# Reordering two second products of an expert around a branch, and making two transposes together

## The chip, the cores and the metric

The kernel runs on one core of one Trainium2 chip. The metric is the device time of one execution in microseconds (us). TensorE is called PE in the profile, its weight loads PEld, VectorE DVE, ScalarE ACT, GpSimd POOL, SyncE SP; a name with a q (PEq, DVEq) is that engine's sequencer, which issues instructions and executes branches.

## The reference

One layer of a decoder for 256 prompt rows and 32 sample rows (288 tokens of 1024 numbers). A convolution and a state-space branch come first; the change lies in what follows them, a mixture of 32 experts, of which each token uses 4:

```python
logits = (t @ w_r + b_r).astype(jnp.float32)
top_val, top_idx = lax.top_k(logits, TOP_K)
gates = jax.nn.softmax(top_val, axis=-1)
for e in range(N_EXPERTS):
    gu = t @ w1[e] + b1[e]
    g = jnp.minimum(gu[:, :D_FF], SWIGLU_LIMIT)
    up = jnp.clip(gu[:, D_FF:], -SWIGLU_LIMIT, SWIGLU_LIMIT)
    act = g * jax.nn.sigmoid(SWIGLU_ALPHA * g) * (up + 1.0)
    out = out + comb[:, e:e + 1] * (act @ w2[e] + b2[e])
```

Everything is float32. An expert's weights are 12 MB, read from memory once; 32 experts are 403 MB.

## The kernel before, in words

`moe` goes through the experts in order. For each it computes only the tokens that were routed to it, in blocks of 32. How many there are is known on the device alone, so the blocks stand under nested branches on a register (`tc.If(reg > 32 * b)`), and every engine takes these branches in its own sequencer. With these inputs 20 experts have at most 32 tokens. Experts 4, 8, 12, 14 and 26 have 33 to 64 (two blocks, 0 and 1); experts 7, 10, 19, 28 and 29 have 65 to 96 (blocks 0 to 2), and 13 and 24 have 129 to 160 (blocks 0 to 4). Blocks 0 and 1 of two neighbouring experts share one tile of 128 rows, `ysp`; blocks from 2 on are the expert's extras and have a tile `ysx` of their own.

A block's work is:

- the gate product `ff1` (line 1216): 68 matmuls on TensorE into one PSUM bank (block 0: bank A; odd blocks: C; even ones: B), and then `silu` on VectorE and ScalarE, which leaves `acts[b]`;
- the transposes `act_tr` (line 1224): two transposes of `acts[b]` on TensorE into bank D and one ScalarE copy into a tile of `ats`;
- the second product `ff2` (line 1234): 64 matmuls (records `y`, line 1243) from `ats` and the second weights into one bank (block 0: C, odd: A, even: B), and then four copies into 32 rows of `ysp` or `ysx` (line 1249), ScalarE and VectorE by turns and one after the other.

`fill` puts a piece of other work in the middle of a product: `{4: ...}` ahead of the fifth of eight steps. `scatter` (line 1257) multiplies `ysp` or `ysx` with a table of gates that VectorE makes (`gates`, line 1251), in matmuls `sc` and `ss` (extras: `sc_x`, `ss_x`), and VectorE adds the result to `acc` and `accs` (lines 1268, 1278).

The order of an expert's work on every engine is written out by hand (the schedule is manual). `ph1` (line 1328): the nest "a" with the gate products of blocks 1 and up, then block 0's gate product with block 1's transposes in it. Then, where `e` is even, the scatter of the two experts before; then the list of the extra tokens of the next expert (`lists`, records `li`, line 1166) and their fetch. `ph2` (line 1341): the nest "b" with the second products of blocks 1 and up:

```python
with tc.If(reg > 32 * b, label=f"{half}{e}_{b}"):
    if b < 5:
        hint(e, reg, half, b + 1)
    end = f(b)
    if b < 5:
        rest(e, reg, half, f, b + 1)
    if end:
        end()
```

Here `f(b)` is block b's second product with the transposes of block b + 1 in its middle, and `end` the scatter of the extras, which block 2 returns. So the order is: product 1, branch on 64, gates and product 2, branch on 96, product 3 and so on, then the scatter. `hint` (line 1307) tells the sequencers ahead of time which way a branch will go (a compare at line 1309 and a hint instruction). In the program a body stands right behind its branch; a branch whose condition doesn't hold goes to a short block behind the body, which only brings the semaphores up to date. After `ph2`: the load of the next expert's count with the first hint for it (`tokens`, line 1311), for even `e` a table of gates and the list of the expert after the next (a one-hot tile `S_None` on VectorE, line 1158, then `li` on TensorE), block 0's transposes, and block 0's second product. Bank C of that product is the one that block 1 of the next expert needs.

SyncE loads the weights in pieces of 1 MB into a ring; a piece's slot is loaded again when the last product that reads it is done (`done`, line 1144). The second weights are released after block 0's second product, which is the last of an expert.

Of the kernel before, what the change touches and what calls it, by code (L numbers as in the profile page):

```python
# [37 lines left out]
NE = 32  # L38
# [1064 lines left out]
def moe(tc, sb, wring, pm, ident, iotaj, h2, h2d, h2off, cm, posm, cnt, b1s3, sel, place, acc, accs, w1, w2, tail, pre, ln_rows, first, final):  # L1103
# [5 lines left out]
    def at_(o, shape, name):  # L1109
        return sb.mem.at(o, shape, F32, name)  # L1110

    def bank(tag, name):
        return pm.tile([P, 512], F32, tag=tag, bufs=1, name=name)
# [4 lines left out]
    acts = [at_(o + 1024 * j, [P, 256], f"acts{2 * i + j}") for i, o in enumerate((o_ac, o_ac2, o_ac2 + 2048)) for j in range(2)]  # L1118
    ats = [at_(o + 1024 * j, [P, 256], f"at{2 * i + j}") for i, o in enumerate((o_sg, o_atx)) for j in range(2)]
# [4 lines left out]
    ysp = at_(o_yp, [P, 1024], "ysp")  # L1124
    ysx = at_(o_y1, [P, 1024], "ysx")
# [61 lines left out]
    def columns_x(nm, m):  # L1187

        r = slice(64 * m, 64 * m + 64)
        tp = pm.tile([P, 8, 64], F32, tag="m", bufs=2, name=f"gt{nm}")  # L1190
        for k in range(8):
            nc.tensor.transpose(tp[:, k], gsx[r, P * k:P * k + P], ident[r, r])
        nc.scalar.copy(htx[:, :, r], tp)

    def silu(nm, a, g, m=0):

        g1 = at_(o_g1 + 1024 * m, [P, 256], f"g1{nm}")
        nc.vector.tensor_scalar_min(g1, g[:, 0:256], 7.0)
        sg = at_(o_sg + 1024 * m, [P, 256], f"sg{nm}")
        nc.scalar.activation(sg, g1, AF.Sigmoid, scale=1.702)  # L1200
        nc.vector.tensor_scalar(a, g[:, 256:512], -7.0, 7.0, op0=ALU.max, op1=ALU.min)
        nc.vector.scalar_tensor_tensor(a, a, 1.0, g1, op0=ALU.add, op1=ALU.mult)
        nc.vector.tensor_tensor(a, a, sg, op=ALU.mult)

    def ff1_mm(e, h, w, outs, fill={}):

        for c, (o, tp) in enumerate(outs):
            nc.tensor.matmul(o, sel[0:96, e:e + 1].to_broadcast([96, w]), b1v[0:96, :, c, :], start=True, stop=False, tile_position=tp)  # L1208
        for k in range(8):
            if k in fill:  # L1210
                fill[k]()
            wk = wt[e][k].rearrange("p u (c n) -> p c u n", c=4)
            for c, (o, tp) in enumerate(outs):
                nc.tensor.matmul(o, h[:, k], wk[:, c], start=False, stop=k == 7, tile_position=tp)

    def ff1(e, b, fill={}):

        gu = bank("ABC"[b and 1 + b % 2], f"gu_{e}_{b}")
        outs = [(gu[32 * c:32 * c + 32, :].rearrange("p (u n) -> p u n", u=2), (0, 32 * c)) for c in range(4)]
        h = htx[:, :, 32 * b - 64:32 * b - 32] if b > 1 else ht[:, :, 64 * (e % 2) + 32 * b:64 * (e % 2) + 32 * b + 32]  # L1220
        ff1_mm(e, h, 32, outs, fill)
        silu(f"_{e}_{b}", acts[b], gu, b % 2)

    def act_tr(nm, bs, tag="D"):

        tp = bank(tag, f"at{nm}")
        for m, (a, t) in enumerate(bs):
            for h in range(2):
                o = 256 * m + 128 * h
                nc.tensor.transpose(tp[:, o:o + P], a[:, h * P:h * P + P], ident)  # L1230
        for m, (a, t) in enumerate(bs):
            nc.scalar.copy(t, tp[:, 256 * m:256 * m + 256])  # L1232

    def ff2(e, b, ys, r, fill={}):

        y = bank("CBA"[b and 1 + b % 2], f"y_{e}_{b}")
        at = ats[b if b < 2 else 2 + b % 2]
        for kt in range(8):
            if kt in fill:
                fill[kt]()  # L1240
            c, h = kt // 2, kt % 2
            for q in range(4):
                nc.tensor.matmul(y[32 * q:32 * q + 32, 0:256], at[:, h * P + 32 * c:h * P + 32 * c + 32],  # L1243
                                 wt[e][8 + c][:, h, 256 * q:256 * q + 256], start=kt == 0, stop=kt == 7, tile_position=(0, 32 * q))
        for q in range(4):
            i, s = slice(32 * q, 32 * q + 32), slice(256 * q, 256 * q + 256)
            if e + 1 == NE and b < 2:
                nc.vector.tensor_tensor(wt[NE][0][r:r + 32, 0, s], y[i, 0:256], wt[NE][1][i, 0, s], op=ALU.mult)  # L1248
            (nc.vector.tensor_copy if q % 2 and b else nc.scalar.copy)(ys[r:r + 32, s], y[i, 0:256])  # L1249

    def gates(o, nm, tab):

        g = at_(o, [P, 288], f"gst{nm}")
        nc.vector.tensor_scalar(g, iotaj[:, 0:288], tab[0][:, 0:1], tab[0][:, 1:2], op0=ALU.is_equal, op1=ALU.mult)
        return g

    def scatter(nm, gst, ys, gated=False):

        for t in range(2):
            for n in range(2):  # L1260
                sc = pm.tile([P, 512], F32, tag="sc", bufs=2, name=f"sc{nm}_{t}_{n}")
                nc.tensor.matmul(sc, gst[:, t * P:t * P + P], ys[:, n * 512:n * 512 + 512], start=True, stop=True)  # L1262
                a = acc[:, t, n * 512:n * 512 + 512]
                if gated:
                    u = at_(o_g1, [P, 512], f"u{nm}_{t}_{n}")
                    nc.vector.tensor_tensor(u, sc, wt[NE][1][:, 0, n * 512:n * 512 + 512], op=ALU.mult)
                    sc = u
                nc.vector.tensor_tensor(a, a, sc, op=ALU.add)  # L1268
        ss = pm.tile([P, 512], F32, tag="sc", bufs=2, name=f"ss{nm}")
        for c in range(4):  # L1270
            nc.tensor.matmul(ss[32 * c:32 * c + 32, 0:256], gst[:, 256:288], ys[:, c * 256:c * 256 + 256],
                             start=True, stop=True, tile_position=(0, 32 * c))
        ss = ss[:, 0:256]
        if gated:
            u = at_(o_atx, [P, 256], f"us{nm}")
            nc.vector.tensor_tensor(u, ss, wt[NE][1][:, 1, 256:512], op=ALU.mult)
            ss = u
        nc.vector.tensor_tensor(accs, accs, ss, op=ALU.add)
# [28 lines left out]
    def hint(e, reg, half, b):  # L1307

        tc.mark_branch_hint_location(f"{half}{e}_{b}", hint=reg > 32 * b, engines=engs)

    def tokens(e):

        reg = nc.values_load(cnt[32:33, e:e + 1], engines=with_pool, min_val=0, max_val=288)
        hint(e, reg, "a", 1)
        return reg

    def rest(e, reg, half, f, b=1):
# [10 lines that stand above are left out]
    def ph1(e, reg):  # L1328

        def f(b):  # L1330
            if b in (2, 4):
                columns_x(f"_{e}_{b}", b // 2 - 1)
            ff1(e, b)
            if b == 5:
                with tc.If(reg > 192):
                    more(e, reg)
        rest(e, reg, "a", f)
        hint(e, reg, "b", 1)
        ff1(e, 0, {5: lambda: act_tr(f"_{e}_1", [(acts[1], ats[1])])})

    def ph2(e, reg):

        def f(b):
            end, fill = None, {}
            if b == 2:
                nm = f"_{e}_x"
                gst = gates(o_g, nm, tabs[2 + e % 2])

                def end():
                    scatter(nm, gst, ysx, e + 1 >= NE)  # L1350
            if b < 5:
                fill[4] = lambda: act_tr(f"_{e}_{b + 1}", [(acts[b + 1], ats[2 + (b + 1) % 2])])
            ff2(e, b, *((ysp, 64 * (e % 2) + 32) if b == 1 else (ysx, 32 * b - 64)), fill)
            return end
        rest(e, reg, "b", f)
        return None if e + 1 == NE else tokens(e + 1)

    steps = pre()
# [8 lines left out]
    with tc.manual_schedule(engines={ENG.PE, ENG.DVE, ENG.Activation, ENG.Pool}):  # L1367
        s, sx = onehot(0, o=o_sg), onehot(0, 64)
        reg = tokens(0)
# [11 lines left out]
        for e in range(NE):  # L1381
            last, j = e + 1 == NE, e // 2
            if not last:
                s = onehot(e + 1, 64)
            ph1(e, reg)
            done(e, range(8))
            if e % 2 == 0 and e:
                scatter(f"_{e}", gst, ysp)
            if not last:
                lists(e + 1, s, tabs[2 + (e + 1) % 2], 0)  # L1390
                fetch(gsx, tabs[2 + (e + 1) % 2])
            reg = ph2(e, reg)
            if e:
                step()
            if e == 1 or e and e % 2 == 0:
                gst = gates(o_gst, f"_{e}", tabs[j % 2])
# [319 lines left out]
```

## Time and profile before

| | |
|---|---|
| Median of 3 runs | 1482.36 us (1478.8 to 1483.93) |
| The profiled execution | 1484.18 us; its span 1482.4 us, 1.8 us lie around it |
[...]
| TensorE busy | 1173.1 us (79% of the span) |
| VectorE, ScalarE, GpSimd busy | 523.7, 298.1, 277.3 us |
| Data moved by DMA | 473.22 MB, mean 319 GB/s |

The first 340 us or so belong to the stage before the experts. In the profile, "idle before" is the time in which an engine did nothing ahead of an instruction, and the name behind the arrow is what ended it. An instruction of which parts overlap its neighbours (matmuls do) has a time that is longer than what it adds to the engine's path; the distance between starts says that. Branches of the sequencers have records of their own, with times; they aren't counted as busy.

### The profile page before, as it was taken

To read this page: it belongs to the slowest core of one execution; us is meant where nothing else is said; L and a number is where in the kernel's file an instruction comes from. 1 tells how busy PE (TensorE), PEld (TensorE's weight loads), DVE (VectorE), ACT (ScalarE), POOL (GpSimd) and SP (SyncE) were. 2 spreads that over 40 slices of the span, in tenths; PEclk is the share of its full clock that TensorE was granted. 3 is DMA by queue.
4 is the path that set the end of the run, shared out by engine and by line. 5 is a ranking of instruction groups with operands and counts; after the bars stand their busy time and mean duration, and the time that the engine had idled before them with its cause. 6 is when DMAs were issued, how large, how long until landed. Compare 5 with 4: busy or idle time off the path is not lost. (4 is left out here: it accounts for less than half of the span.)

```text
span 1482.4 us, 25892 instructions
## 1 busy us (share of the span) xinstructions
PE 1173.1 (79%) x10262; PEld 592.5 (40%) x10262; DVE 523.7 (35%) x1057; ACT 298.1 (20%) x624; POOL 277.3 (19%) x237
## 2 busy tenths in 40 slices
PE   4888788886778768888779977778777897778975
PEld 0777677853323323333323433333323233223332
DVE  6789898752222122212221321212202122213124
ACT  2634645520101101111101111111011011111111
POOL 4676865621100000000000000000000000000022
PEclk8889889997799789989889998889888998999998
DMA  9465646578799999998793589999999957997683
GB/s 393 164 228 147 221 148 244 216 288 318 283 414 413 411 413 414 380 364 346 308 398 120 229 342 363 412 413 412 414 414 412 381 230 282 414 415 283 262 334 125
DMA packets 91769, 473.22 MB, mean 319 GB/s; under 512 B 14406, under 2 KB 15774, under 8 KB 52560
## 3 DMA queue, kind: packets, MB, share of 16 engines
q1 hardware_dynamic: 81264, 459.68, 78.1%
q0 software_dynamic: 7328, 6.55, 1.6%
q8 instruction: 167, 2.74, 0.7%
q10 hardware_dynamic: 2912, 3.46, 0.7%
q14 instruction: 98, 0.80, 0.2%
HBM read 485.33 MB, written 4.28 MB: 330 GB/s over the span
## 5 line engine op out<-in xcount | busy, mean ns | idle before, releaser
L1176 POOL DMA_INDIRECT gs1.360_2956<-h2d,tab3.366_2962 x16 | 15.9, 993 | 558.9 <-DVE tab3.366_2962 L1172 350.9
L1249 ACT COPY ysp.368_2964<-y 32x256 f32<-32x256 f32 x152 | 55.2, 363 | 186.5 <-PE y L1243 173.9
L1176 POOL DMA_INDIRECT gs1.360_2956<-h2d,tab2.365_2961 x16 | 16.0, 1001 | 344.7 <-DVE tab2.365_2961 L1172 154.5
L1208 PE MATMUL gu<-b1h.19_79,sel.17_76 96*32 96x512 bf16 x220 | 23.2, 410 | 71.9 <-PEq L1319 44.2
L567 DVE SCALAR_TENSOR_TENSOR v.103_627<-cb.73_324,pk.20_89,v.103_627 128x256 f32<-128x256 f32 x60 | 54.7, 911 | 1.5
L1232 ACT COPY at1.356_2952<-at 128x256 f32<-128x256 f32 x32 | 11.9, 372 | 206.8 <-PE at L1230 206.8
L1232 ACT COPY at0.355_2951<-at 128x256 f32<-128x256 f32 x32 | 11.9, 373 | 200.2 <-PE at L1230 199.7
L1230 PE MATMUL at<-consts.1_57,acts0.349_2945 128*128 128x128 f32 x64 | 17.7, 371 | 39.8 <-issue 32.0
L1208 PEld LDWEIGHTS <-sel.17_76 96*32 96x32 bf16 x220 | 7.0, 93 | 97.7 <-issue 96.1
L1268 DVE TENSOR_TENSOR acc.345_2940<-acc.345_2940,sc 128x512 f32<-128x512 f32 x60 | 39.8, 683 | 11.9 <-PE sc L1262 11.9
L1268 DVE TENSOR_TENSOR acc.345_2940<-acc.345_2940,sc_x 128x512 f32<-128x512 f32 x28 | 19.2, 687 | 27.3 <-PE sc_x L1262 27.3
L1249 DVE COPY ysp.368_2964<-y 32x256 f32<-32x256 f32 x24 | 10.2, 423 | 52.6 <-ACT ysp.368_2964 L1249 52.6
L1185 DVE COPY ht.361_2957<-gt 128x512 f32<-128x512 f32 x16 | 11.1, 692 | 49.9 <-PE gt L1184 49.9
L1230 PEld LDWEIGHTS at<-consts.1_57,acts0.349_2945 128*128 128x128 f32 x64 | 10.4, 212 | 43.2 <-issue 38.9
L1184 PE MATMUL gt<-consts.1_57,gs0.359_2955 128*128 128x128 f32 x120 | 23.6, 362 | 0.0
L1176 POOL DMA_INDIRECT gs0.359_2955<-h2d,tab1.364_2960 x8 | 7.9, 991 | 78.2 <-DVE tab1.364_2960 L1168 70.6
L1184 PEld LDWEIGHTS gt<-consts.1_57,gs0.359_2955 128*128 128x128 f32 x120 | 20.7, 193 | 0.3 <-issue 0.2
L1249 DVE COPY ysx.369_2965<-y 32x256 f32<-32x256 f32 x22 | 9.3, 421 | 30.7 <-ACT ysx.369_2965 L1249 30.7
L1232 ACT COPY at2.357_2953<-at 128x256 f32<-128x256 f32 x14 | 5.2, 372 | 70.7 <-PE at L1230 70.7
L1230 PEld LDWEIGHTS at<-consts.1_57,acts1.350_2946 128*128 128x128 f32 x64 | 6.4, 141 | 26.8 <-issue 26.8
L1176 POOL DMA_INDIRECT gs0.359_2955<-h2d,tab0.363_2959 x7 | 6.9, 992 | 48.1 <-DVE tab0.363_2959 L1168 48.1
L1230 PE MATMUL at<-consts.1_57,acts1.350_2946 128*128 128x128 f32 x64 | 14.0, 301 | 0.0
(3009 smaller groups left out, 2946.5 us busy)
## 6 DMA issues: line engine op xcount, KB each, us to landing
wada_0.21_91<-in_w_ada_dram SPq DMA_DIRECT2D x1, 1024.0 KB
wada_1.22_93<-in_w_ada_dram SPq DMA_DIRECT2D x1, 1024.0 KB
wada_2.24_97<-in_w_ada_dram SPq DMA_DIRECT2D x1, 1024.0 KB
wada_3.25_99<-in_w_ada_dram SPq DMA_DIRECT2D x1, 1024.0 KB, 12.7
wada_4.26_101<-in_w_ada_dram SPq DMA_DIRECT2D x1, 1024.0 KB
wada_5.27_103<-in_w_ada_dram SPq DMA_DIRECT2D x1, 1024.0 KB
wada_6.28_105<-in_w_ada_dram SPq DMA_DIRECT2D x1, 1024.0 KB
wada_7.29_107<-in_w_ada_dram SPq DMA_DIRECT2D x1, 1024.0 KB
```

The source lines that it names most:

```text
L567: V.scalar_tensor_tensor(vt_(j), cb[:, j, k:k + 256], wd[:, k, j:j + 1], vt_(j), op0=ALU.mult, op1=ALU.add)
L1176: nc.gpsimd.indirect_dma_start(out=g, out_offset=None, in_=h2d, in_offset=bass.IndirectOffsetOnAxis(ap=tab[1], axis=0), bounds_check=287, ...
L1184: nc.tensor.transpose(tp[:, i], gs[:, P * (4 * h + i):P * (4 * h + i) + P], ident)
L1185: (nc.vector.tensor_copy if h else nc.scalar.copy)(ht[:, 4 * h:4 * h + 4], tp)
L1208: nc.tensor.matmul(o, sel[0:96, e:e + 1].to_broadcast([96, w]), b1v[0:96, :, c, :], start=True, stop=False, tile_position=tp)
L1230: nc.tensor.transpose(tp[:, o:o + P], a[:, h * P:h * P + P], ident)
L1232: nc.scalar.copy(t, tp[:, 256 * m:256 * m + 256])
L1249: (nc.vector.tensor_copy if q % 2 and b else nc.scalar.copy)(ys[r:r + 32, s], y[i, 0:256])
L1268: nc.vector.tensor_tensor(a, a, sc, op=ALU.add)
```

## The change

Block 1's transposes, which lay in block 0's gate product, now take block 2's with them (`acts[1:3]` into `ats[1:3]`), for every expert, whether it has a block 2 or not. The nest "b" becomes: branch on 32, then at once the branch on 64. If there are more than 64 tokens: gates, product 2, the branches on 96 and up with their products, then block 1's second product, and then the scatter of the extras. If there are not: an else arm with block 1's second product alone. That product now stands twice in the program and has no transposes in it.

```diff
-        ff1(e, 0, {5: lambda: act_tr(f"_{e}_1", [(acts[1], ats[1])])})
+        ff1(e, 0, {5: lambda: act_tr(f"_{e}_1", list(zip(acts[1:3], ats[1:3])))})
 
     def ph2(e, reg):
 
+        def first():
+            ff2(e, 1, ysp, 64 * (e % 2) + 32)
+
         def f(b):
-            end, fill = None, {}
-            if b == 2:
+            fill = {}
+            if b < 5:
+                fill[4] = lambda: act_tr(f"_{e}_{b + 1}", [(acts[b + 1], ats[2 + (b + 1) % 2])])
+            ff2(e, b, ysx, 32 * b - 64, fill)
+
+        with tc.If(reg > 32, label=f"b{e}_1"):
+            hint(e, reg, "b", 2)
+            with tc.If(reg > 64, label=f"b{e}_2") as two:
+                hint(e, reg, "b", 3)
                 nm = f"_{e}_x"
                 gst = gates(o_g, nm, tabs[2 + e % 2])
-
-                def end():
-                    scatter(nm, gst, ysx, e + 1 >= NE)
-            if b < 5:
-                fill[4] = lambda: act_tr(f"_{e}_{b + 1}", [(acts[b + 1], ats[2 + (b + 1) % 2])])
-            ff2(e, b, *((ysp, 64 * (e % 2) + 32) if b == 1 else (ysx, 32 * b - 64)), fill)
-            return end
-        rest(e, reg, "b", f)
+                f(2)
+                rest(e, reg, "b", f, 3)
+                first()
+                scatter(nm, gst, ysx, e + 1 >= NE)
+            with two.Else():
+                first()
         return None if e + 1 == NE else tokens(e + 1)
```

## Rows read from the trace of the kernel before

**Rows 1.** The page: slices of the span, busy tenths; a group of section 5.

```profile
DMA  9465646578799999998793589999999957997683
...
L1268 DVE TENSOR_TENSOR acc.345_2940<-acc.345_2940,sc_x 128x512 f32<-128x512 f32 x28 | 19.2, 687 | 27.3 <-PE sc_x L1262 27.3
```

**Rows 2.** Stretches: length, busy us by engine (instructions), clock, DMA share, GB/s.

```profile
851.00:1151.00 300.00, 231.46 (x2072) 96.97 (x2068) 61.85 (x166) 35.67 (x92) 14.87 (x15) 0.87 0.98 396
```

**Rows 3.** Waits of TensorE, 400 to 1482 us: total, times, longest.

```profile
PE gu L1208 <- PEq L1319: 43.3, 22, 5.0
PE at L1230 <- issue: 32.0, 9, 4.1
...
PE sc_x L1262 <- PEq L1319: 11.8, 3, 4.5
...
PE sc_x L1262 <- DVEq L1319: 8.0, 4, 2.1
...
PE gu L1214 <- DMA w_7.640_9292<-in_w_dram: 1.5, 1, 1.5
```

**Rows 4.** Branches of line 1319, 400 to 1482 us: ns shortest/median/longest, first and last start.

```profile
L1319 PEldq COMPARE_BRANCH  x132: 67/192/6258, 397.9 to 1453.0; - x132
```

**Rows 5.** Timeline of TensorE, expert 8, around block 1's second product: start, us, work.

```profile
621.29 1.07 PE L1243 MATMUL y<-w_8.679_10236,at1.356_2952 128*32 128x256 f32 x16
...
623.15 0.44 PE L1230 MATMUL at<-consts.1_57,acts2.351_2947 128*128 128x128 f32 x2
...
624.41 1.05 PE L1243 MATMUL y<-w_11.682_10242,at1.356_2952 128*32 128x256 f32 x16
629.10 1.44 PE L1166 MATMUL li<-cm.14_73,S_None.724_11485 128*128 128x4 f32 x6 [3.64 <-DVE S_None.724_11485 L1158]
```

**Rows 6.** The branch on 64 alone, experts 4, 8, 12, 14, 26: ns, start.

```profile
L1319 PEldq COMPARE_BRANCH  x1: 2483/2483/2483, 475.9 to 475.9; - x1
L1319 PEldq COMPARE_BRANCH  x1: 2791/2791/2791, 624.0 to 624.0; - x1
L1319 PEldq COMPARE_BRANCH  x1: 4383/4383/4383, 770.4 to 770.4; - x1
L1319 PEldq COMPARE_BRANCH  x1: 6236/6236/6236, 880.1 to 880.1; - x1
L1319 PEldq COMPARE_BRANCH  x1: 4232/4232/4232, 1283.2 to 1283.2; - x1
```

**Rows 7.** Expert 8: branches from 619 to 628 us; the hint's compare.

```profile
L1319 PEldq COMPARE_BRANCH  x3: 83/192/2791, 620.0 to 627.0; - x3
...
L1309 PEldq ALU_OP  x1: 37/37/37, 620.2 to 620.2; - x1
```

**Rows 8.** Timeline of VectorE, expert 8, behind block 1's second product.

```profile
625.91 0.42 DVE L1249 COPY ysp.368_2964<-y 32x256 f32<-32x256 f32 x1 [4.11 <-ACT ysp.368_2964 L1249]
...
628.49 0.55 DVE L1158 TENSOR_TENSOR S_None.724_11485<-consts.1_57,posm.15_74 128x384 f32<-128x384 f32 x1
```

**Rows 9.** Timeline of TensorE, products and scatter of the extras, experts 7 and 29.

```profile
574.71 1.07 PE L1243 MATMUL y<-w_8.641_9294,at1.356_2952 128*32 128x256 f32 x16 [0.37 <-ACT sg_0.677_10229 L1200]
...
581.79 1.05 PE L1243 MATMUL y<-w_11.644_9300,at2.357_2953 128*32 128x256 f32 x16
586.95 5.43 PE L1262 MATMUL sc_x<-ysx.369_2965,gst_x.686_10321 128*128 128x512 f32 x8 [4.11 <-PEq L1319]
...
1411.06 3.86 PE L1262 MATMUL sc_x<-ysx.369_2965,gst_x.1500_30827 128*128 128x512 f32 x8 [1.94 <-DVEq L1319]
```

**Rows 10.** Timeline of TensorE, the list behind block 1's product, experts 4, 12, 14, 26.

```profile
480.96 1.45 PE L1166 MATMUL li<-cm.14_73,S_None.576_7759 128*128 128x4 f32 x6 [3.62 <-DVE S_None.576_7759 L1158]
...
776.20 1.43 PE L1166 MATMUL li<-cm.14_73,S_None.872_15211 128*128 128x4 f32 x6 [4.30 <-DVE S_None.872_15211 L1158]
...
887.71 1.44 PE L1166 MATMUL li<-cm.14_73,S_None.946_17074 128*128 128x4 f32 x6 [6.15 <-DVE S_None.946_17074 L1158]
...
1288.83 0.82 PE L1166 MATMUL li<-cm.14_73,S_None.1390_28252 128*128 128x4 f32 x6 [4.13 <-DVE S_None.1390_28252 L1158]
```

## The prediction

> **What bounds the kernel now.** I read the page's slices first, then the stretches, then TensorE's waits, then single branches. In the expert stage the DMA engines are full in many slices [rows 1], 98% busy over the 300 us of experts 14 to 23 [rows 2]. Yet TensorE almost never waits for a weight: of its waits after 400 us the largest on a DMA is 1.5 us [rows 3], and with the smaller ones, all at experts 6, 7 and 24, I count some 7 us. So TensorE's own order sets the pace, and the ring of weights can take up about 7 us of any delay. What TensorE does wait for is its sequencer at the branches: 43.3 us before a first matmul of the next gate product, 32.0 us ahead of transposes with no other cause shown, and 11.8 + 8.0 us before the scatter of extra sums [rows 3].
>
> A branch of PE's sequencer takes between 67 and 6258 ns, median 192 [rows 4]. The short ones fall through into the block that stands next; the long ones skip a block of code. Row by row, the branch on 64 tokens in the five experts with 33 to 64 tokens took 2.5, 2.8, 4.4, 6.2 and 4.2 us [rows 6]. It is issued some 4 us after its hint: for expert 8 the hint's compare stands at 620.2 [rows 7] and the branch at 624.0 [rows 6], the second product lying between. So the target arrived 6.4 to 10.2 us after the hint. That is the quantity on which all else rests.
>
> **Part 1: the else arm, experts 4, 8, 12, 14, 26.** Before, the branch on 64 waits behind the second product. TensorE works through that product meanwhile (623.15 to 625.46 is its second half), and the next list starts at 629.10, after 3.64 us of waiting for VectorE [rows 5]. That wait is VectorE's: its copies of the product begin at 625.91 and its one-hot ends at 629.04 [rows 8], so about 3.5 us follow any second product, whatever the branch does. After the change the hint stands where it stood, but the branch on 64 follows it at once, and the product stands behind the branch. The code arrives when it did before; what covered the wait now comes after it. Expert 8: branch end 624.0 + 2.8 = 626.8, then the product. Two of these take 574.71 to 582.84, 8.1 us [rows 9], so 4.1 each, less 0.4 for the transposes no longer in it. I add 1.5 because TensorE has idled: the scatter that followed a 4.11 us gap took 5.43 us, one after 1.94 us took 3.86 [rows 9], and I take that difference for the product as an estimate. With 0.3 us of starting and 3.6 of VectorE the next list comes 9.1 us after the branch's end: 635.9 instead of 629.10, +6.8. In the same way expert 4: 475.9 + 2.5 + 9.1 = 487.5 instead of 480.96, +6.5; expert 12: +7.7; 14: +7.7; 26: +7.7 [rows 6, 10]. Sum 36.4 us. Some comes back: the next expert's first branch gets its hint earlier against TensorE's work, and a part of the 43.3 us [rows 3] lies there; I estimate 6 us for experts 5, 9 and 27. Net +30. Bounds: without the cold clock 7 less; with a second block of code that has to arrive in the middle of the product, up to some 2 us each, 10 more.
>
> [...]
>
> **Part 2: the other arm, experts 7, 10, 13, 19, 24, 28, 29** (28 additions, four each [rows 1]). The scatter's matmul waited 4.11 us in expert 7 and 1.94 in expert 29 [rows 9]; over the seven it is 11.8 + 8.0 = 19.8 us [rows 3]. About 2 us of each is the copies of the last extra product, which the change lays under the moved product; the rest is the branch on 96, which stays between the products and now leaves its gap ahead of the moved one. Its hint moves 4 us earlier, as does the work behind it, and in odd experts somewhat more, since the sequencer runs ahead there. I keep 8 us of gaps (2 in expert 7, 3 in 10, 1 in 19, 2 in 28) and so save 12. The odd experts also lose a wait of 0.4 us ahead of the second product, as that product's bank is the first gate product's: 4 x 0.4, some 2 us. Saved 14; bounds 5 (only experts 13, 24 and part of 29 win) and 24 (all gaps go and the scatter runs warm). The other queues cost nothing: no list, DMA issue or weight release changes its place, and VectorE's table of gates only moves ahead of a product for which it waits anyway.
>
> At the end of this arm a jump over the else body is new, seven times. Nothing in the trace shows one of that length by itself; between 0.2 us (the median branch) and 2.5 (the shortest of the five above) I take 0.3, as the skipped code is one product long and the code behind it follows in order: 2 us, bounds 1 and 17.
>
> **Part 3: transposes made together.** Two transposes cost TensorE 0.4 us [rows 5]. In the 12 larger experts they move. In the other 20 they are new, with one ScalarE copy that nothing waits for. In the 12 odd ones TensorE then waits for a branch anyway (the 32.0 us [rows 3]); the 8 even ones pay: 3 us. If that cover is gone, 7 us.
>
> **Sum.** 30 - 14 + 2 + 3 = 21, less 7 us that the ring takes up (TensorE's waits for weights shrink by that): +14. The profiled execution took 1484.2 us, its span 1482.4; the median of the runs shown is 1.8 us below it. 1484.2 + 14 = 1498; between the two bases I say 1497.
>
> **Rivals.** *The branch is cheap (faster).* If the else arm is at hand when the branch comes, or arrives within the 1.3 us that the sequencer is ahead (in expert 8 its branch on 32 stands at 620.0 [rows 7], the product behind it at 621.29 [rows 5]), the five experts pay nothing: their waits for the list, 3.6 + 3.6 + 4.3 + 6.1 + 4.1 us [rows 5, 10], shrink to 3.5 each (-4), the transposes leave (-2), hints come earlier (-6). With -14 and +3 that is -23: 1461. It decides wherever the stall is under about 2 us. Against it: all five branches to that target were longer. For it: the target lies elsewhere in the new code. [...] Chance 0.13.
>
> *The fetch starts at the branch, not at the hint (no change).* The branch comes 4 us earlier than it did, so the code also does, and part 1 falls by 20 to 10 us: 10 - 14 + 2 + 3 - 3 = -2, 1482. For it: expert 14's branch alone took 6.2 us. Against: the branches of experts 4 and 8 ended 2.5 and 2.8 us after their start, too soon for a fetch that began with them, if 6.2 us is one. Chance 0.18.
>
> *Second fetches (slower still).* The else product straddles a block in most of the five, and the new jump stalls in all seven: +10 and +15, 1522. Chance 0.17. My forecast keeps 0.52.
>
> **Numbers.** A measurement of this kernel tells about 0.3% (4.5 us) from no change. The range 1470 to 1524 leaves out most of the first rival and the tail of the last; the likeliest case alone spans 1484 to 1515. Slower: 0.17 + 0.47; same: 0.12 + 0.05; the rest, 0.19, faster.
>
> **What would show it.** In the changed profile TensorE's second product in experts 4, 8, 12, 14 and 26 has an idle time of 5 to 9 us before it, put down to PE's sequencer, and some branches of 6 to 10 us; the waits for the list stay at 3.5. The scatter's matmuls wait for nothing, and gaps of 0 to 3 us stand ahead of the moved product. If the second product of those five experts starts right behind the list, part 1 is wrong and the first rival holds.

## The result and the profile after

The changed kernel takes 1532.84 us (median of 4 runs, 1528.49 to 1534.52) against 1482.49 us before (4 runs): a ratio of 1.0308, 95% interval 1.0269 to 1.0348. It is slower, as forecast, but by 50 us where 15 were forecast, and outside the range by 9 us. The profiled execution took 1528.49 us, its span is 1526.7 us; that is 44.3 us more than the span before, and these 44.3 us are what is to be found below.

First the page. TensorE's line, the DMA slices, the instruction queue (q8: packets, MB, share) and VectorE's additions of the extras:

```profile
PE 1184.1 (78%) x10302; PEld 603.2 (40%) x10302; DVE 523.3 (34%) x1057; ACT 301.8 (20%) x644; POOL 277.5 (18%) x237
...
DMA  9457456567999998697992669999999849995681
...
q8 instruction: 174, 2.85, 0.8%
...
L1268 DVE TENSOR_TENSOR acc.345_2940<-acc.345_2940,sc_x 128x512 f32<-128x512 f32 x28 | 18.6, 686 | 5.8 <-PE sc_x L1262 5.5
```

TensorE is busy 11 us longer (1173.1 before) on the same matmuls and 40 more small transposes. The run with the transposes alone (below) is busy for 1177.0 us, so some 7 us of the 11 are matmuls that took longer; in the five products behind the else arm (below) the granted clock was 0.50 to 0.80 of full speed. The DMA slices look as they did [rows 1]; there is no new transfer, but 7 more instruction packets (167 before). VectorE's idle time ahead of the extras fell from 27.3 us [rows 1] to 5.8: that wait of the scatter is indeed gone.

Next, TensorE's waits from 400 us on (total, times, longest):

```profile
PE gu L1208 <- PEq L1319: 41.3, 22, 5.1
PE at L1230 <- issue: 29.4, 9, 4.0
PE y L1243 <- issue: 28.0, 9, 5.5
...
PE y L1243 <- PEq L1319: 11.7, 4, 4.8
PE gu L1214 <- issue: 10.2, 6, 3.1
...
PE y L1243 <- DVEq L1319: 5.8, 3, 1.9
PE gt L1184 <- issue: 5.7, 2, 3.0
PE y L1243 <- DMA w_4.540_7017<-in_w_dram: 5.6, 1, 5.6
...
PE y L1243 <- DMA w_0.719_11456<-in_w_dram: 5.5, 1, 5.5
PE y L1243 <- DMA w_0.941_17261<-in_w_dram: 5.4, 1, 5.4
...
PE sc_x L1262 <- DVE acc.345_2940 L1268: 4.4, 7, 0.7
...
PE gu L1214 <- DMA w_7.530_6619<-in_w_dram: 0.7, 1, 0.7
```

Before, the rows of "issue" ahead of the gate and second products were:

```profile
PE gu L1214 <- issue: 6.0, 3, 2.8
...
PE y L1243 <- issue: 3.5, 3, 1.3
```

Read against [rows 3]: the 19.8 us of `sc_x` on sequencers are gone, 4.4 us on VectorE's additions are left. In their place `y` waits, which before had only those 3.5 us of "issue" and no wait for a sequencer or a DMA. Five of these waits, 5.4 to 5.6 us each, stand ahead of block 1's product in experts 4, 8, 12, 14 and 26; three of the five carry the name of a weight's DMA, two are among the nine of "issue". The name of the DMA is only the last event that the profile saw. The branches on 64 show the cause, one row for each of the five:

```profile
L1354 PEldq COMPARE_BRANCH  x1: 6282/6282/6282, 471.4 to 471.4; - x1
L1354 PEldq COMPARE_BRANCH  x1: 6257/6257/6257, 626.0 to 626.0; - x1
L1354 PEldq COMPARE_BRANCH  x1: 6250/6250/6250, 771.4 to 771.4; - x1
L1354 PEldq COMPARE_BRANCH  x1: 6112/6112/6112, 891.3 to 891.3; - x1
L1354 PEldq COMPARE_BRANCH  x1: 6077/6077/6077, 1300.1 to 1300.1; - x1
```

Each took 6.1 to 6.3 us, against 2.5 to 6.2 before [rows 6], and each product begins some 0.3 us behind its branch. In each of these waits one packet of the instruction queue lands, about 1.5 us before the branch ends (in expert 8 at 630.7, the branch's end at 632.3, in the trace's packet records). In the larger experts, where the same branch goes on to the next block, it took 0.07 us (the trace's branch records).

TensorE's timeline in expert 4, from the list ahead of block 1's product to the list behind it:

```profile
471.52 0.83 PE L1166 MATMUL li<-cm.14_73,S_64.543_7023 128*128 128x2 f32 x6
477.90 1.93 PE L1243 MATMUL y<-w_8.531_6621,at1.356_2952 128*32 128x256 f32 x16 [5.56 <-DMA w_4.540_7017<-in_w_dram]
...
483.00 1.26 PE L1243 MATMUL y<-w_11.534_6627,at1.356_2952 128*32 128x256 f32 x16
487.32 1.44 PE L1166 MATMUL li<-cm.14_73,S_None.576_7939 128*128 128x4 f32 x6 [3.06 <-DVE S_None.576_7939 L1158]
```

The product starts 5.56 us late, takes 6.4 us from 477.90 to the end of its last row at 484.26, and then the wait of 3.06 us for VectorE's one-hot stands where it stood [rows 10]. The granted clock of that product (a stretch: length, PE, PEld, DVE, ACT, POOL busy, clock, DMA share, GB/s):

```profile
477.90:484.30 6.40, 6.35 (x64) 3.15 (x64) 0.00 (x0) 0.00 (x0) 0.00 (x0) 0.57 1.01 412
```

Behind an idle time of 5.56 us the granted clock is 0.57 of full speed, near the lower of the two levels in the trace's clock records, 0.5 and 1; the same product without a gap ahead took 3.7 us at a granted clock of 1.00 in another kernel (arms swapped, below), so the cold clock costs 2.7 us and not the 1.5 estimated.

In the larger arm, the moved product of expert 28:

```profile
1383.65 0.64 PE L1243 MATMUL y<-w_8.1419_29841,at1.356_2952 128*32 128x256 f32 x8 [2.25 <-PEq L1319]
1389.14 1.08 PE L1243 MATMUL y<-w_8.1419_29841,at1.356_2952 128*32 128x256 f32 x8 [4.85 <-issue]
```

The moved product waits 2.25 us for the branch on 96, runs 8 matmuls, and then stops for 4.85 us in the middle with no cause but "issue": a packet on the instruction queue ended 1.4 us before it went on. The same happened in experts 19 (4.17 us) and 7 (1.22), and in the else product of experts 8 (2.09) and 26 (1.59). Stops inside a group, all rows of "issue" but the one ahead of `at`, less the two gaps of 5.5 and 5.4 counted above: 28.0 - 10.9 + 10.2 + 5.7 = 33 us, against 6.0 + 3.5 = 9.5 us before.

Last, where the moved product of expert 13 waits:

```profile
852.22 1.07 PE L1243 MATMUL y<-w_8.863_15318,at1.356_2952 128*32 128x256 f32 x16 [1.94 <-DVEq L1319]
```

It waits for VectorE's sequencer and not for a branch of TensorE's own; experts 10 and 24 have the same row. (In expert 10 TensorE's own branch on 96, of 2.83 us, ended only 0.6 us earlier, so there VectorE adds little.) The product writes to bank A, which blocks 3 and 5 use inside the nest; so at the nest's end TensorE waits for VectorE, whose last work before that is to copy the extra product out (in expert 13 until 852.02). This is the wait that the scatter had [rows 9], moved one product ahead.

**The sum.** Idle time on TensorE: five gaps +27.3, the moved product's waits 11.7 + 5.8 = +17.5, stops inside groups +23.5; scatter -15.4, lists of the five 21.7 to 15.5 [rows 5, 10], -6.2; weights 7.0 to 0.7, -6.3; gate products and transposes behind a branch 75.3 to 70.7, -4.6. With 11 us more of busy time that is +46.8, and 44.3 were measured; the 2.5 us between are smaller waits that were not summed.

The same by place, which the experiments are compared by: stretch E is from the list ahead of block 1's product to the next list, summed over the five experts with an else arm (46.5 us before); stretch L is from the first second product of the nest to the end of the scatter of extras, over the seven larger experts (130.3 us before). Both are differences of starts and ends in TensorE's timeline, as shown for expert 4 (471.52 to 487.32: 15.8 us; before 472.42 to 480.96: 8.5). The span is given against 1482.4 us. All three are of one profiled execution each, which can lie some us off its kernel's median (that of "else arm alone" and that of "bank C, hint lost" are the slowest of their kernels). The kernel before was timed again beside the runs below and took 1486 to 1488 us there, so their span column holds 3 to 6 us that are not theirs; the ratio compares with these times, and what is said of faster and slower goes by it. Block 2's transposes lay in E and L before and lie in neither after (nor in "transposes alone"): a second product took 4.16 us with them (expert 8) and takes 3.66 without, so waits and stops grew by some 0.5 us more in each of the 12 experts than E and L show. With that, two kernels that can't be told from the one before, transposes alone and code shifted, show how far the sums stray: E by 1 us, L by 5.

| kernel | E | L | span | time ratio, interval |
|---|---|---|---|---|
| the change | +36.6 | +10.4 | +44.3 | 1.0308, 1.0269 to 1.0348 |
| transposes alone | -2.9 | +1.6 | +9.8 | 1.0024, 0.9985 to 1.0064 |
| else arm alone | +43.2 | -5.3 | +50.6 | 1.0241, 1.0200 to 1.0282 |
| change, bank C | +34.5 | +10.4 | +41.4 | 1.0257, 1.0215 to 1.0299 |
| before, code shifted | +0.9 | +4.8 | +10.7 | 1.0023, 0.9995 to 1.0051 |
| change, early hint | +25.4 | +16.8 | +38.7 | 1.0245, 1.0212 to 1.0279 |
| early hint, bank C | +13.4 | +6.8 | +14.3 | 1.0123, 1.0097 to 1.0150 |
| both hints early, bank C | +24.4 | +24.5 | +46.0 | 1.0268, 1.0244 to 1.0291 |
| change, arms swapped | +5.5 | +22.2 | +37.1 | 1.0222, 1.0181 to 1.0262 |
| bank C, hint lost | +37.0 | +19.2 | +72.1 | 1.0373, 1.0307 to 1.0438 |
| before, early hint | +8.0 | +14.0 | +22.6 | 1.0109, 1.0074 to 1.0144 |
| bank C, product joined | +40.5 | +2.7 | +38.6 | 1.0232, 1.0171 to 1.0293 |

### The profile page after: what moved, and what is told of

Its sections match the earlier page's. It is cut to its first block, busy times and chain, and to the rows that moved or that the text cites. A ratio compares the mean times of both kernels' runs of the same rounds, so it can differ in the third digit from the quotient of the medians.

```text
span 1526.7 us, 25981 instructions
## 1 busy us (share of the span) xinstructions
PE 1184.1 (78%) x10302; PEld 603.2 (40%) x10302; DVE 523.3 (34%) x1057; ACT 301.8 (20%) x644; POOL 277.5 (18%) x237
## 5 line engine op out<-in xcount | busy, mean ns | idle before, releaser
L1249 DVE COPY ysp.368_2964<-y 32x256 f32<-32x256 f32 x24 | 10.2, 423 | 120.7 <-ACT ysp.368_2964 L1249 120.7
L1184 PE MATMUL gt<-consts.1_57,gs0.359_2955 128*128 128x128 f32 x120 | 22.6, 346 | 5.7 <-issue 5.7
L1201 DVE TENSOR_SCALAR acts0.349_2945<-gu 128x256 f32<-128x256 f32 x32 | 13.3, 415 | 0.0
```

The costliest lines, as they stand in the source:

```text
L1184: nc.tensor.transpose(tp[:, i], gs[:, P * (4 * h + i):P * (4 * h + i) + P], ident)
```

## The experiments

The theory behind them: the else arm's far jump costs most, and what is moved in the larger arm hides nothing. The rivals: the transposes, the new layout of the code as such, the bank alone, or the second copy of the product.

**Transposes alone.** Of the change only the common transposes; the old order of the products and their single copy stay. Against the changed kernel:

```diff
             hint(e, reg, "b", 2)
+            first()
             with tc.If(reg > 64, label=f"b{e}_2") as two:
...
-                first()
                 scatter(nm, gst, ysx, e + 1 >= NE)
-            with two.Else():
-                first()
```

> Only the transposes are made together; block 1's product stands ahead of the branch on 64 again and there is no else arm. Theory 1 (the far else arm carries the loss): 1482 + 3 = 1485 us (1478 to 1492), and the sum of the waits ahead of the lists and of the scatter as before, 22 and 20 us. Rival (a shifted program and more transposes carry it): over 1500 us.

1.0024, the interval holding 1 (10 runs). The lists of the five wait 21.4 us, as expected, the scatter 24.8 where 20 were expected. The term of +3 us (1.002) stands within what can be told; the transposes are not the loss.

**Else arm alone.** Against the changed kernel: block 1's product stands first in both arms, so the larger experts keep the old order.

```diff
         with tc.If(reg > 32, label=f"b{e}_1"):
             hint(e, reg, "b", 2)
             with tc.If(reg > 64, label=f"b{e}_2") as two:
...
+                first()
                 f(2)
                 rest(e, reg, "b", f, 3)
-                first()
                 scatter(nm, gst, ysx, e + 1 >= NE)
             with two.Else():
                 first()
```

> Both arms begin with block 1's product, so only the branch on 64 moves ahead of it; the scatter waits as before. Theory 1: the five experts of the else arm still idle 5 to 5.6 us each ahead of block 1's product, 27 us in all, and 1505 to 1518 us. Rival (the else arm is cheap, the moved product costs): under 1492 us, with those waits under 2 us.

1.0241: some 36 us of the 46 that the change's ratio stands for come with the else arm, E at +43.2. The five gaps are 5.3 to 5.8 us, as the theory has it, and the else product stops in its middle besides, for 3.6 us in expert 8 and 3.9 in 26. The scatter's waits are back, 19.6 us as before [rows 3]:

```profile
PE sc_x L1262 <- PEq L1319: 9.9, 2, 5.1
PE sc_x L1262 <- DVEq L1319: 9.7, 5, 1.9
```

**Bank C for the moved product.** The theory: without bank A it doesn't wait for VectorE at the join.

```diff
-    def ff2(e, b, ys, r, fill={}):
+    def ff2(e, b, ys, r, fill={}, tag=None):
-        y = bank("CBA"[b and 1 + b % 2], f"y_{e}_{b}")
+        y = bank(tag or "CBA"[b and 1 + b % 2], f"y_{e}_{b}")
...
-                first()
+                first("C")
```

> As the change, but the moved product of the larger arm goes into bank C instead of A, which a block 3 or 5 within the nest may have used. Theory (where the nest joins, TensorE's next use of bank A waits for VectorE's whole nest, the extra copies with it, so the move hides nothing): the waits of 1.9 us ahead of the moved product in experts 10, 13 and 24 go, some 6 to 9 us in all, 1524 to 1528 us. Rival (the branch alone makes the wait): 1531 to 1535 us and the waits as in the change.

The wait on VectorE's sequencer is gone from the view of waits. In experts 13 and 24 the product now waits 0.47 us instead of 1.94; in expert 10 it waits about as long as in the change (2.14 us, 1.94 there), now for TensorE's own branch on 96. All waits of the moved product stand under one name:

```profile
PE y L1243 <- PEq L1319: 14.9, 7, 4.8
```

That is 14.9 us in seven experts, where the change has 11.7 in four and 5.8 in three: 2.6 us less. L stays at +10.4, as the product of expert 10 then runs longer (5.35 us, 3.66 in the change). The intervals of this kernel (1.0215 to 1.0299) and of the change (1.0269 to 1.0348) overlap. So the bank's wait was real and small; nearly all that is left stands behind the branch on 96.

**Code shifted.** The kernel before, with 64 unused one-column matmuls ahead of the expert loop, so that all later code stands at another place in the program.

```diff
+        z = pm.tile([P, 512], F32, tag="m", bufs=2, name="shift")
+        for _ in range(64):
+            nc.tensor.matmul(z[0:32, 0:1], sel[:, 0:32], sel[:, 0:1], start=True, stop=True)
```

> [...] Theory 1 (where the program's blocks fall matters little): 1480 to 1490 us. Rival (the place of the blocks decides tens of us, and with it much of the change's loss): 1495 us or more, or under 1475, with the waits in the middle of products at other places and 8 us or more apart in sum.

1.0023, the interval holding 1. Stops inside groups change place; their rows are

```profile
PE gu L1214 <- issue: 13.2, 7, 3.2
...
PE y L1243 <- issue: 1.3, 1, 1.3
```

14.5 us in sum against 9.5 before, where the change has 33. So this one other place of the code does not make stops like the change's; others were not tried.

**Early hint.** The hint for the branch on 64 stands 0.1 us ahead of it in the change. Here it is given at the end of the branch on 32 in the nest of gate products, some 13 us earlier.

```diff
+            if b == 1:
+                return lambda: hint(e, reg, "b", 2)
         rest(e, reg, "a", f)
...
         with tc.If(reg > 32, label=f"b{e}_1"):
-            hint(e, reg, "b", 2)
             with tc.If(reg > 64, label=f"b{e}_2") as two:
```

> The changed kernel with one hint moved: the hint for the branch on 64 is given a whole gate product of block 0 earlier, inside the nest of the gate products (by the end of its branch on 32), and no longer between the branch on 32 and the branch on 64. Theory (the code of the else arm arrives a fixed time after its hint, so an earlier hint brings it in time): the five idle times of 5.4 to 5.6 us (27.3 us in sum) ahead of block 1's product in experts 4, 8, 12, 14 and 26 vanish or fall below 1 us each; the time falls by 20 to 35 us to about 1498 to 1512. Rival (the fetch begins at the branch, or what was hinted is lost again to the code that is fetched in between): the five idle times stay at 5 to 6 us and the time stays at about 1530.

Neither side held: in expert 8 alone the gap vanished, in the other four it stayed at 5.2 to 5.9 us, and the time came to 1.0245.

**Early hint and bank C.** The two edits above together.

> The kernel with the earlier hint, and in the larger arm block 1's product takes bank C, as in the run on the bank. Theory: the gains add: the five idle times vanish and the wait for VectorE ahead of the moved product too; about 7 us below the kernel with the earlier hint alone, 1490 to 1505. Rival (the branch on 96 then sets the start of the moved product in all seven larger experts): no difference from the kernel with the earlier hint.

1.0123, 27 us less than the change by the ratios, and the best kernel with an else arm. The branches on 64 of experts 4, 8, 12, 14 and 26:

```profile
L1355 PEldq COMPARE_BRANCH  x1: 6042/6042/6042, 471.0 to 471.0; - x1
L1355 PEldq COMPARE_BRANCH  x1: 380/380/380, 625.3 to 625.3; - x1
L1355 PEldq COMPARE_BRANCH  x1: 367/367/367, 760.5 to 760.5; - x1
L1355 PEldq COMPARE_BRANCH  x1: 6537/6537/6537, 873.5 to 873.5; - x1
L1355 PEldq COMPARE_BRANCH  x1: 362/362/362, 1278.4 to 1278.4; - x1
```

Three of five are short, and there the product follows the list at once, 16 matmuls in 1.07 us, as in arms swapped (below) at a granted clock of 1.00; expert 12:

```profile
760.84 0.83 PE L1166 MATMUL li<-cm.14_73,S_64.839_14691 128*128 128x2 f32 x6
761.60 1.07 PE L1243 MATMUL y<-w_8.827_14298,at1.356_2952 128*32 128x256 f32 x16
...
764.22 0.61 PE L1243 MATMUL y<-w_11.830_14304,at1.356_2952 128*32 128x256 f32 x7
```

Even so each of the three products stops once in its middle, for 3.23, 1.81 and 2.24 us in experts 8, 12 and 26; in the last line above the last step breaks off behind 7 of 16 matmuls. E falls from +36.6 to +13.4: +2.5, +0.5 and +1.5 in these three, +5.5 and +3.4 in experts 4 and 14. That is the clearest evidence for the jump: same arms, same order, and most of the loss goes where the code has arrived. Two of the five still took 6.0 and 6.5 us with the same hint. In the three, two instruction packets ended within 6 us after the hint; in the two, the second ended 7 to 10 us after it. That the running product's own next block took the fetch's place there is a guess.

**Both hints early, bank C.** Also the branch on 96 is hinted early.

```diff
-            if b == 1:
-                return lambda: hint(e, reg, "b", 2)
+            if b < 3:
+                return lambda: hint(e, reg, "b", b + 1)
...
-                hint(e, reg, "b", 3)
```

> As the run before, and the hint for the branch on 96 is also given early, by the end of the branch on 64 in the nest of the gate products. Theory: the idle times ahead of the moved product (15 us over five experts with bank C) fall below 5 us; the time is 1480 to 1495, near the kernel before or below it. Rival (only the last hint counts, one fetch in flight at a time): the second hint spoils the first, the five idle times of 5.5 us or those ahead of the moved product stay, and the time is no better than that of the run before.

The rival's outcome came, but not for its reason: four gaps are back (5.2 to 6.1 us), the larger arms are worse (L +24.5), 1.0268. The added hint stands under the branch on 64, so the five experts with a gap never execute it; each has the same two hints ahead of its branch as in the run before. What the edit changed for them is the place of the code.

**Arms swapped.** The else body stands right behind the branch, the larger arm behind it.

```diff
-            with tc.If(reg > 64, label=f"b{e}_2") as two:
+            with tc.If(reg > 64, preferred_fallthrough_block=False, label=f"b{e}_2") as two:
```

> The changed kernel with the two arms exchanged in the program: the else body (block 1's product) stands right behind the branch on 64, and the larger arm lies behind it and is reached by a jump over one product. Theory (what costs is the way to code that isn't next): the five idle times of 5.5 us vanish, at the end of the else body a jump over the larger arm stalls instead, but about 3 us of that stall lie beside VectorE's copies and one-hot; the seven larger experts stall at the branch on 64 by up to 6 us each. Sum: -27 + 10 + 20 or so, about 1525 to 1535 if all seven stall, 1500 to 1515 if none does. Rival (the fetch is needed for either arm, wherever it stands): the five idle times stay, 1530 to 1560.

All five gaps vanish, but the jump over the larger arm, now at the end of the else body, takes 6.0 to 6.3 us and delays the list. None of the seven larger experts stalls at the branch on 64, where the theory had up to 6 us each: their jump over the else body, one product long, took 0.21 to 0.42 us (the trace's branch records). What they pay is some 5 us more often at the branch on 96. Waits, and the timeline of expert 4:

```profile
PE li L1166 <- issue: 29.8, 5, 6.1
PE y L1243 <- PEq L1319: 23.0, 5, 5.1
```

```profile
470.77 1.07 PE L1243 MATMUL y<-w_8.531_6621,at1.356_2952 128*32 128x256 f32 x16
...
473.38 1.05 PE L1243 MATMUL y<-w_11.534_6627,at1.356_2952 128*32 128x256 f32 x16
480.38 1.44 PE L1166 MATMUL li<-cm.14_73,S_None.576_7939 128*128 128x4 f32 x6 [5.95 <-issue]
```

The product takes 3.7 us (470.77 to 474.43) and the list comes 5.95 us later, of which 3.06 are VectorE's in any case. E is +5.5, L +22.2, and 1.0222 stands for 1515 us, the upper end of what was expected without stalls at that branch. So the far jump's cost in the five is about half covered; why the branch on 96 then costs the larger experts more was not tested.

**Hint in the middle of the gate product.** Meant to give the hint for the branch on 64 later than in the runs above, with bank C.

```diff
+        ff1(e, 0, {2: lambda: hint(e, reg, "b", 2),
+                   5: lambda: act_tr(f"_{e}_1", list(zip(acts[1:3], ats[1:3])))})
...
-            hint(e, reg, "b", 2)
             with tc.If(reg > 64, label=f"b{e}_2") as two:
```

> The kernel with bank C for the moved product; the hint for the branch on 64 is given in the middle of block 0's gate product (ahead of its third step, for every expert), some 10 us before the branch and 2 us behind the hint for the branch on 32. Theory (a hinted block arrives if nothing else has to be fetched between the hint and the branch, as in three of five experts of the run before): in at least three of experts 4, 8, 12, 14 and 26 the idle time ahead of block 1's product vanishes (from 5.5 us), and the time is 1495 to 1515. Rival (the fetch that the running product itself needs comes after the hint and takes its place): three or more of the five idle times stay at 5 to 6 us and the time is 1515 to 1535; the 20 small experts, which never come to this branch, lose a fetch each besides and may be slower still.

It tests something else. TensorE's hints here, and with bank C alone:

```profile
L1720 PEldq BRANCH_PREFETCH_HINT  x98: 27/35/46, 331.5 to 1517.0; - x98
```

```profile
L1720 PEldq BRANCH_PREFETCH_HINT  x110: 28/35/50, 326.3 to 1488.8; - x110
```

Twelve are missing, one for each expert that comes to the branch on 64: no such hint was executed. So this is the change with bank C and without that hint. The five gaps are 5.1 to 5.9 us, as with it: a hint 0.1 us ahead was worth nothing there. The larger arms lose (L +19.2 against +10.4), and 1.0373 is the slowest of all; some 16 us of its span lie in neither stretch and weren't traced to a cause.

**Early hint in the old order.** The kernel before, with only the hint moved up.

```diff
+            if b == 1:
+                return lambda: hint(e, reg, "b", 2)
         rest(e, reg, "a", f)
...
-            if b < 5:
+            if b < 5 and (half, b) != ("b", 1):
                 hint(e, reg, half, b + 1)
```

> The kernel before, with the hint for the branch on 64 given a gate product earlier, as in the run with the earlier hint; the order of the work is the old one. Theory (in the old order the branch on 64 waits beside VectorE's copies and one-hot, so nothing is to be won): the waits for the list fall at most from 21.7 to some 16 us over the five experts, the larger experts' scatter still waits for 8 us or more, and the time is that of before within 0.4%. Rival (the branches of the sequencer are what sets the time everywhere, and an earlier hint shortens them): 1465 to 1478.

Slower, 1.0109, which neither side expected. The scatter waits 30.7 us where it waited 19.8 [rows 3], and the lists of the five wait 5.9 to 6.1 us where they waited 3.6 to 6.1 [rows 5, 10]; the first of them and the scatter's rows:

```profile
PE sc_x L1262 <- DVEq L1319: 17.3, 4, 7.1
PE sc_x L1262 <- PEq L1319: 13.4, 3, 4.7
...
PE li L1166 <- DVE S_None.576_7729 L1158: 5.9, 1, 5.9
```

With a product between hint and branch the branches on 64 of the five took 2.5 to 6.2 us in the old order [rows 6]; with a gate product, a scatter and another hint between, those of experts 4 and 8 took 5.9 and 6.0 (2.5 and 2.8 before).

**Product joined.** No else arm: the product stands once, behind the body of the branch on 64, and the scatter under a branch of its own.

```diff
                 rest(e, reg, "b", f, 3)
-                first("C")
-                scatter(nm, gst, ysx, e + 1 >= NE)
-            with two.Else():
-                first()
+            first("C")
+            with tc.If(reg > 64):
+                scatter(nm, gst, ysx, e + 1 >= NE)
```

> The kernel with bank C for the moved product, without an else arm: block 1's product stands once, behind the body of the branch on 64, and the scatter of the extras stands behind it under a branch on 64 of its own. So the five experts with 33 to 64 tokens jump over the larger arm to the same product, and then over the scatter. Theory (what costs is a branch with nothing beside it, whatever is behind it): five idle times of 5 to 6 us ahead of block 1's product as in the change; the second product is in the program once, so fewer stalls in the middle of groups; 1510 to 1527. Rival (the copy of the product in an else arm, apart from the other code, is what costs): the idle times fall to 0 to 3 us, and the time is below 1500.

Five gaps of 5.3 to 5.9 us again, three of them under a weight's name, two under the branch on 64:

```profile
PE y L1243 <- PEq L1355: 11.0, 2, 5.6
...
PE y L1243 <- DMA w_0.941_16757<-in_w_dram: 5.9, 1, 5.9
...
PE y L1243 <- DMA w_0.719_11168<-in_w_dram: 5.3, 1, 5.3
```

1.0232, as the theory has it. The second copy of the product is not the cause: the jump over the larger arm with nothing beside it costs the same with one copy of the product (5.3 to 5.9 us) as with two (5.4 to 5.6).

No version beats the kernel before.

## Why the prediction was right in sign and wrong in size

**Part 1 was right in its sum, by luck.** 36.4 us were worked out for the five experts, E measured +36.6. Expert by expert it was 7.3, 10.6, 6.7, 4.6 and 7.5 against 6.5, 6.8, 7.7, 7.7 and 7.7. Three terms inside were off and offset each other. The branch ended 5.9 to 6.1 us after the start of the list ahead of it, where the rows of before had given 5.9, 6.3, 7.9, 9.7 and 7.7: some 7 us less in sum. So the arrival after the hint, with the hint right ahead of the branch, is the low end of what was taken for it. The product took some 10 us more than forecast: the cold clock costs 2.7 us rather than 1.5, and experts 8 and 26 stop in mid-product (2.09 and 1.59 us), as the upper bound had it. The wait for the list is 3.06 us instead of 3.6, 2.7 us less in sum; in 14 it had been 6.15 [rows 10], as it was the branch's too. The mechanism was right all the same: in the early-hint kernels most of the loss goes where this wait goes.

**Part 2 is the step that failed**: "about 2 us of each is the copies of the last extra product, which the change lays under the moved product", and the 14 us saved that follow. L measured +10.4, a miss of 22 us with the 2 us for the jump. The scatter's waits did fall by 15.4 us. But the moved product itself waits 17.5 us where 8 were kept: 4.85 us in expert 7 and 1.9 to 2.4 in each of the other six, three of which (13, 24, 29) had been given no wait at all. In experts 13 and 24 that is VectorE through bank A (the run with bank C brought it from 1.94 to 0.47 us), in the others the branch on 96 (in expert 10 both). So a moved piece of work covers a wait only if it doesn't end up behind the same wait; the prediction looked up the bank's conflict at the old place and not at the new one. Then the stops in mid-product of experts 7, 19 and 28, 10.2 us, which the prediction had priced only for the else arm and the jump. The instruction packets that end 1.4 us before such a product goes on speak for a fetch as the cause; no run tested it. Of the 30 us between the sum of the prediction (+14) and the span (+44.3), part 2 makes 22 and what did not come back (below) 7.

**The jump over the else body** at 2 us was right: the seven branches took 0.20 to 0.31 us, 2.0 in sum (the trace's branch records).

**Part 3** at +3 us agrees with 1.0024, which can't be told from nothing, and with TensorE's busy time there, 3.9 us longer.

**What comes back.** The ring took up 6.3 us (7 said). The branches behind gave back 4.6 over all experts; 6 were said for experts 5, 9 and 27 alone, where it is 2.5. Outside E and L only 2.7 us came back, where -6 + 3 - 7 = -10 had been summed. Against it stand new stops: 5.7 us ahead of the `gt` for experts 6 and 22, and 4.2 more in gate products. And in expert 30 a branch on 32 took 6.04 us where it took 0.46 (the trace's branch records), for which a gate product waits 4.98 us instead of 0.41; the 4.6 above has this loss in it. It follows expert 29's larger arm directly; that such arms put off the fetches behind them is argued and not tested.

**The rivals.** "The branch is cheap" fell with the five rows of 6.1 to 6.3 us. "The fetch starts at the branch" can't be told from the forecast in this kernel, as hint and branch are 0.1 us apart; the run without the hint shows that for the five it makes no difference. Of the 20 us by which it had part 1 fall, the earlier arrival gave some 7, and the slower product took them back. "Second fetches" (1522) was the nearest and deserved more than 0.17. Its places were half right: stops in the else product and none at the jump, but also in the moved product. Of the signs, the idle times (5.4 to 5.6 us), the long branches and the scatter came as said; the idle times stand under other names than PE's sequencer, and the gaps ahead of the moved product reach 4.85 us instead of 3.

## What to carry over

A jump over the larger arm costs TensorE 6 us in this kernel, one over a single product 0.2 to 0.4. What the long one really costs is set by the work in the engine's queue at that moment (in expert 8 the branch of 2.79 us before ran beside a product and VectorE's copies, that of 6.26 us in the change left a gap of 5.52): before moving work across such a branch, ask what will run while the code comes. Before laying work under a wait, check that its own buffers and branches don't put it behind that same wait. Bodies behind a jump can also stop in their middle (33 us in the change against 9.5 of such stops before), so leave room for that in the sum.

## What the runs showed of the hardware

- Without an early hint, the time of a jump went by what it jumped over. Over one product it took 0.20 to 0.31 us (the change, seven times, over the else body) and 0.21 to 0.42 (arms swapped, seven times), over the larger arm 6.1 to 6.3 (the change) and 6.0 to 6.3 (arms swapped), five times each.
- A hint can make things worse. Given some 13 us ahead instead of right ahead, it brought the code in one of five experts, with the product in another bank in three, with the branch on 96 hinted early too in one, and in the old order in none (all five waits 5.9 to 6.1 us, and the kernel 1.1% slower). What decides between arrival and loss stayed open. One thing goes with it: the branch that stands 0.1 us behind the early hint took 0.45 us in the five cases where the code arrived and 0.20 to 0.21 in the fifteen where it didn't (the trace's branch records).
- A product of 64 matmuls can stop for 1.2 to 4.9 us in its middle (the change), with "issue" as its only cause, when it was reached by a jump.
- The same edit's time hangs on small differences of the code: early hint with and without bank C differ by 1.2% (1.0123 and 1.0245). Of 24 us between their spans, 12 lie in E, by which of the five branches find their code, and 10 in L.
